# The last gathers ahead of the overflow loop, and a closing norm in two operations a tile

## Chip, cores and metric

One core of a Trainium2 chip runs the program. The metric is the device time of one execution in microseconds (us), as the median of three timed runs. The profile is one more execution, taken with the hardware profiler.

## What is computed

The reference is a network of two blocks over 512 tokens of width 1024, in float32. The first block is attention with a convolution beside it, and then a layer of product-key experts (PEER). The second block has two layers; the second of them ends with a mixture of eight experts (MoE), each token going to two of them, a weighted residual and a layer norm. Only that end is touched here:

```python
def _layernorm(x, g, b):
    xf = x.astype(jnp.float32)
    mu = jnp.mean(xf, axis=-1, keepdims=True)
    var = jnp.mean(jnp.square(xf - mu), axis=-1, keepdims=True)
    return ((xf - mu) * lax.rsqrt(var + LN_EPS) * g.astype(jnp.float32)
            + b.astype(jnp.float32)).astype(x.dtype)

ff = _moe_swiglu(u, w_router, w_gate, w_up, w_down)
x = _layernorm(DEEPNORM_ALPHA * x + (1.0 + g2) * ff, ln2_g[layer], ln2_b[layer])
```

## The kernel before

TensorE (PE) does the matmuls, in three passes of split float32 operands; ScalarE (ACT) and VectorE (DVE) make the splits of the streamed weights (L126, L128); SyncE (SP) issues most transfers; GpSimd (POOL) issues indirect transfers and some small work. The order on PE is the program's own. For the other engines a list scheduler puts the instructions in order when the program is built, and each engine then runs its list in that order.

In `moe` (it ends at L1735) the tokens are written to a buffer in DRAM in rows sorted by expert. A loop over the eight experts (L1700 on) calls `more_rows` or `few_rows`; each result leaves by `store_rows` (L1801: DVE scales it into the tile `yrow`; L1802: POOL stores it to `ybuf`). There are two buffers `ybuf`, one for each half of 512 columns.

The function `gather(h)` (from L1684) brings half h back to token order: for each of the four tiles of 128 tokens two indirect transfers on POOL's queue (L1691, one for each of the token's two experts) into the tile `y`, and two adds on DVE into the residual tile `xt` (L1694, 128x512, one scalar and two tensors). `gather(0)` is called while the last expert's second half is still being multiplied. `gather(1)` needs the store of that second half.

Between the two stands `dense_experts` (L1931, L1932): a loop for tokens that find no room in an expert's rows. Its trip count is read at run time: every engine loads it from the tile `route` (TENSOR_LOAD, L1931) and branches over the loop's body if it is 0, as it is in the runs here. Behind the body stands a block in which each engine waits for the semaphores of all others and of all transfers, before it goes on. The scheduler moves nothing across this loop.

Behind it come `gather(1)`, the statistics of each half row (L1721, `bn_stats`, 8 of them), and the closing norm, two tiles at a time: `bn_aggr` (L1727), an inverse root of 11 small DVE operations (`rsqrt`, L248 to L254), the negated product of mean and root (L1730), then for each tile ACT's scale and shift (L1732), DVE's product with the gain (L1733), DVE's sum with the shift (L1734), all 128x1024, and one store of 512 KB (L1735).

Of the kernel before, what the change touches and what calls it, by code (L numbers as in the profile page):

```python
# [17 lines left out]
AF = mybir.ActivationFunctionType  # L18
OP = mybir.AluOpType
AX = mybir.AxisListType  # L20

P = 128
# [3 lines left out]
NT = 4  # L26
# [1089 lines left out]
LN_EPS = 1e-5  # L1116
# [354 lines left out]
def moe(N, x, acc, last, m2):  # L1471
# [4 lines left out]
    nc, I, sb, tc = N.nc, N.I, N.sb, N.tc  # L1476
    V, A, PE, G = nc.vector, nc.scalar, nc.tensor, nc.gpsimd
# [30 lines left out]
    rows = N.slab([P, 4, D], F32, "rows")  # L1508
# [22 lines left out]
    def area(n, dt=F32):  # L1531
        a = w[:, at[0]:at[0] + n]
        at[0] += n
        return a if dt == F32 else a.bitcast(dt)
# [43 lines left out]
    for t in range(NT):  # L1578
        s = slice(t * NE, (t + 1) * NE)
# [74 lines left out]
    for i in range(2):  # L1654
        for t in range(NT):
            s = G.indirect_dma_start(out=xbuf, out_offset=bass.IndirectOffsetOnAxis(ap=put[:, i, t:t + 1], axis=0),
                                     in_=ut[:, t], in_offset=None, bounds_check=NROWS - 1, oob_is_err=False)
# [24 lines left out]
    xr = [xt[:, t] for t in range(NT)]  # L1682
    bn = area(48).rearrange("p (t h s) -> p t h s", t=NT, h=2)

    def gather(h):

        y = N.slab([P, NT, 2, 512], name="y")
        s = slice(h * 512, (h + 1) * 512)
        for t in range(NT):
            for i in range(2):  # L1690
                G.indirect_dma_start(out=y[:, t, i], out_offset=None, in_=ybuf[h],  # L1691
                                     in_offset=bass.IndirectOffsetOnAxis(ap=get[:, i, t:t + 1], axis=0))
            for i in range(2):
                V.scalar_tensor_tensor(xr[t][:, s], y[:, t, i], gw[:, i, t:t + 1], xr[t][:, s], OP.mult, OP.add)  # L1694
# [19 lines left out]
        behind = late  # L1714
    for f in behind:
        f()
    dense_experts(N, ints[0:1, NE:NE + 1], ud, wd, rows, xr)
    gather(1)
    for t in range(NT):
        for h in range(2):  # L1720
            V.bn_stats(bn[:, t, h], xr[t][:, h * 512:(h + 1) * 512])  # L1721


    mv = area(16).rearrange("p (t s) -> p t s", t=NT)
    for t0 in range(0, NT, 2):
        for t in (t0, t0 + 1):
            V.bn_aggr(mv[:, t, 0:2], bn[:, t])  # L1727
        m = mv[:, t0:t0 + 2]
        rs = N.rsqrt(m[:, :, 1], 2, 1.0, LN_EPS)
        V.scalar_tensor_tensor(m[:, :, 2], m[:, :, 0], -1.0, rs, OP.mult, OP.mult)  # L1730
        for t in (t0, t0 + 1):
            A.activation(xr[t], xr[t], AF.Identity, scale=rs[:, t - t0:t - t0 + 1], bias=mv[:, t, 2:3])  # L1732
            V.tensor_mul(xr[t], xr[t], rows[:, 1])  # L1733
            V.tensor_add(xr[t], xr[t], rows[:, 2])  # L1734
            nc.sync.dma_start(I["out"][t * P:(t + 1) * P], xr[t])  # L1735


def rows_now(N, ut, row, iota):
# [183 lines left out]
def dense_experts(N, trips, ud, wd, rows, xr):  # L1922

    nc, tc, I = N.nc, N.tc, N.I
    V, A, PE, G = nc.vector, nc.scalar, nc.tensor, nc.gpsimd
    y = N.slab([P, KT, T], F32, "dy")
    gu, down = (I["moe_" + k].rearrange("e a p n -> (e a) p n") for k in ("gu", "down"))
    H = 256
    uu = N.slab([P, 2, KT, H], F32R, "du")
    hs = [N.slab([P, 2, 8, H], F32R, "dh") for _ in range(3)]  # L1930
    n = nc.values_load(trips, min_val=0, max_val=NE)  # L1931
    with tc.For_i(0, n) as e:  # L1932
        for hf in range(2):
            ts = slice(hf * H, (hf + 1) * H)
            for k in range(0, KT, 2):
                t = N.tmp([P, 2, H], name="du")
                nc.sync.dma_start(t, ud[:, k:k + 2, ts])
                N.cut(uu[:, 0, k:k + 2], uu[:, 1, k:k + 2], t)
            wr = N.tmp([P, 512], name="dw")
            nc.sync.dma_start(wr[:, 0:H], wd[bass.ds(e, 1), ts].to_broadcast([P, H]))  # L1940
            for f in range(NF):
                ps = [N.ps(), N.ps()]
                for q in range(2):
                    wh, wl = N.split(N.raw_at(gu, e * NF + f, q * 1024))
                    for k in range(4):
                        kk = 4 * q + k
                        for i in range(2):
                            s = slice((2 * k + i) * P, (2 * k + i + 1) * P)
                            N.mm3(ps[i][:, 0:H], wh[:, s], wl[:, s], uu[:, 0, kk], uu[:, 1, kk], kk == 0, kk == KT - 1)
                t = N.tmp([P, 512], name="dg")  # L1950
                A.activation(t[:, 0:H], ps[0][:, 0:H], AF.Silu)
                h = hs[f // 8]
                V.tensor_mul(t[:, 0:H], t[:, 0:H], ps[1][:, 0:H])
                N.cut(h[:, 0, f % 8], h[:, 1, f % 8], t[:, 0:H])
            for q in range(4):
                ps = [N.ps(), N.ps()]
                for a in range(3):
                    m = min(8, NF - 8 * a)
                    for b in range(0, m, 4):
                        wh, wl = N.split(N.raw_at(down, e * 12 + q * 3 + a, b * 256, min(4, m - b) * 256))  # L1960
                        for j in range(min(4, m - b)):
                            f = 8 * a + b + j
                            for i in range(2):
                                s = slice((2 * j + i) * P, (2 * j + i + 1) * P)
                                h = hs[f // 8]
                                N.mm3(ps[i][:, 0:H], wh[:, s], wl[:, s], h[:, 0, f % 8], h[:, 1, f % 8], f == 0, f == NF - 1)
                for i in range(2):
                    V.tensor_mul(y[:, 2 * q + i, ts], ps[i][:, 0:H], wr[:, 0:H])
        for t in range(NT):
            for h in range(2):  # L1970
                p, s = N.ps(), slice(h * 512, (h + 1) * 512)
                for k in range(4):
                    PE.transpose(p[:, k * P:(k + 1) * P], y[:, 4 * h + k, t * P:(t + 1) * P], N.ident)
                r = N.tmp([P, 512], name="yrow")
                V.tensor_mul(r, p, rows[:, 0, s])
                V.tensor_add(xr[t][:, s], xr[t][:, s], r)
# [161 lines left out]
def build(tc, nc, I):  # L2138
    with ExitStack() as ctx:
        N = Net(ctx, tc, I)  # L2140
        N.setup()
        with tc.manual_schedule(engines={mybir.EngineType.PE}):
            with tc.tile_pool(name="early", bufs=1) as N.gp:
                N.gv = N.gp
                x, mods, late, last = mixer1(N)
                (m0, gem0), (m1, gem1) = (modulation(N, l) for l in range(2))
                x, last = peer(N, x, mods, last, (late, gem0(0, 16)))
                start = enter(N, x, last, m0)
            late = ExitStack()
            N.gp = N.late = late.enter_context(tc.tile_pool(name="late", bufs=1))  # L2150
            N.nraw = 6
            N.second()
            with tc.tile_pool(name="gemv", bufs=1) as N.gv:
                N.background("gemv", gem0(16, 48), 2)
                acc, last = mixer2(N, 0, x, *start, m0)
                start = next_input(N, x, acc, last, (0, 4, 7), N.v("ln1_g0"), N.v("ln1_b0"), m0[:, 32:40], m0[:, 24:32])
                N.background("gemv", gem1(0, 48), 1)
                x, acc, last = ffn(N, x, *start, m0)
                N.drain("gemv")
            start = next_input(N, x, acc, last, (0, 2, 3), N.v("ln2_g0"), N.v("ln2_b0"), m1[:, 8:16], m1[:, 0:8])  # L2160
            acc, last = mixer2(N, 1, x, *start, m1)
            late.close()
            N.gp = N.mp = ctx.enter_context(tc.tile_pool(name="moe", bufs=1))
            N.nraw = MOE_RAW
            moe(N, x, acc, last, m1)
# [11 lines left out]
```

## Time and profile before

| what | value |
|---|---|
| median of 3 timed runs | 3920.79 us (3920.43 to 3928.07) |
| time of the profiled execution | 3927.0 us |
| its span, first to last instruction | 3925.1 us |
| PE busy | 3646.8 us, 93% |
| DVE busy | 2897.0 us, 74% |
| ACT busy | 1733.0 us, 44% |
| POOL busy | 989.9 us, 25% |

Times in the rows count from the span's start. The last matmul of the program ends about 36 us before the span does, so what the change touches lies in a stretch in which PE is idle. The profiled execution took 1.9 us more than its span, and 6.2 us more than the median of the timed runs.

### The profile page before, as it was taken

The page shows a single profiled execution, that of the slowest core. Times are in us where ns is not written, and L with a number is a line of the kernel's source. Part 1 is how long each engine was busy: PE and PEld are TensorE (multiplying, and loading weights), DVE is VectorE, ACT ScalarE, POOL GpSimd, SP SyncE. Part 2 cuts the span into 40 slices and gives each one's busy share as a digit, 9 for nine tenths or more (in the row PEclk, how much of TensorE's full clock was granted, in tenths as well). Part 3 has the DMA queues.
Part 4 walks back from the last instruction along what each step waited for, and adds up shares of the span by engine and source line. Part 5 has one row for each costly group of instructions (what it writes and reads, how often), then busy time and mean ns, then how long its engine had stood idle before and what let it go on. Part 6 is the DMA issues. An engine that isn't in the chain of part 4 may idle for free.

```text
span 3925.1 us, 61947 instructions
## 1 busy us (share of the span) xinstructions
PE 3646.8 (93%) x23129; PEld 3331.8 (85%) x23129; DVE 2897.0 (74%) x4938; ACT 1733.0 (44%) x2697; POOL 989.9 (25%) x936
## 2 busy tenths in 40 slices
PE   8999899987999778989999899999999999999996
PEld 5877778887999678889898788888889999999996
DVE  6799866999689766767855755554455788888898
ACT  3355543332444222323333223222324678787775
POOL 2212111054032344555523021002103304031211
PEclk9999999998999889999998999999998999999998
DMA  5322253389599988778864625663124799999997
GB/s 217 98 68 97 95 198 111 102 313 340 179 320 334 360 310 297 288 289 295 303 232 147 193 96 168 188 198 102 60 94 184 262 335 331 339 341 339 338 349 256
DMA packets 314758, 898.97 MB, mean 229 GB/s; under 512 B 28179, under 2 KB 114451, under 8 KB 312783
## 3 DMA queue, kind: packets, MB, share of 16 engines
q1 hardware_dynamic: 273583, 747.68, 55.7%
q0 software_dynamic: 40864, 147.25, 9.9%
q8 instruction: 183, 3.00, 0.3%
q14 instruction: 128, 1.05, 0.1%
HBM read 816.35 MB, written 78.46 MB: 228 GB/s over the span
## 4 chain that ended last, share of the span: by engine, by line
PE 39%; DMA 9%; DVE 6%; issue 5%; POOL 3%; ACT 2%; SPq 0%; DVEq 0%; POOLq 0%; ACTq 0%
PE ps L1819 10%; PE ps L154 9%; PE ps L155 9%; PE ps L153 9%; DMA gw<-Wd 3%; DVE wl L128 2%; DMA raw<-in_peer_v_dram 2%; ACT wh L126 1%; DMA rows<-in_peer_urows_dram,own 1%; DMA raw<-in_ada_w_dram 1%; DVE cw L139 1%; POOL gw L1066 1%; DMA rows<-in_peer_vrows_dram,own 1%; POOL mod L312 1%; DVE raw L331 1%
## 5 line engine op out<-in xcount | busy, mean ns | idle before, releaser
L126 ACT ACTIVATE wh<-raw 128x1024 fp32r<-128x1024 f32 (+1 forms) x1014 | 1050.2, 1042 | 1131.1 <-PE ps L154 594.9
L128 DVE TENSOR_TENSOR wl<-raw,wh 128x1024 fp32r<-128x1024 f32 (+1 forms) x1000 | 1221.5, 1235 | 310.9 <-ACT wh L126 295.0
L155 PE MATMUL ps<-h2h,wl 128*128 128x384 f32 (+2 forms) x1176 | 413.6, 352 | 46.1 <-DVE wl L128 46.1
L153 PE MATMUL ps<-h2h,wh 128*128 128x384 f32 (+2 forms) x1176 | 420.8, 358 | 32.1 <-ACT wh L126 27.7
L155 PE MATMUL ps<-cw,wl 128*128 128x384 f32 (+2 forms) x1088 | 376.0, 346 | 47.2 <-DVE wl L128 47.1
L154 PE MATMUL ps<-h2l,wh 128*128 128x384 f32 (+2 forms) x1176 | 410.2, 349 | 2.3 <-DVE h2l L139 2.1
L153 PE MATMUL ps<-cw,wh 128*128 128x384 f32 (+2 forms) x1088 | 372.5, 342 | 15.9 <-ACT wh L126 15.9
L154 PE MATMUL ps<-cw,wh 128*128 128x384 f32 (+2 forms) x1088 | 371.3, 341 | 0.0
L155 PEld LDWEIGHTS ps<-h2h,wl 128*128 128x128 f32 x1176 | 229.0, 195 | 59.9 <-DVE wl L128 55.1
L154 PE MATMUL ps<-ul,wh 128*128 128x512 f32 (+1 forms) x712 | 269.7, 379 | 8.5 <-DVE ul L139 7.8
L926 POOL DMA_INDIRECT rows<-in_peer_urows_dram,own x128 | 183.6, 1435 | 368.9 <-issue 203.4
L153 PE MATMUL ps<-uh,wh 128*128 128x512 f32 (+1 forms) x712 | 272.6, 383 | 3.4 <-ACT uh L138 2.3
L155 PE MATMUL ps<-uh,wl 128*128 128x512 f32 (+1 forms) x712 | 267.3, 375 | 0.0
L155 PEld LDWEIGHTS ps<-cw,wl 128*128 128x128 f32 x1088 | 215.7, 198 | 58.1 <-DVE wl L128 58.0
L153 PEld LDWEIGHTS ps<-h2h,wh 128*128 128x128 f32 x1176 | 229.6, 195 | 40.2 <-ACT wh L126 30.9
L331 DVE SCALAR_TENSOR_TENSOR raw<-raw,over 128x1024 f32<-128x1024 f32 x128 | 158.5, 1245 | 129.5 <-DMA raw<-in_ada_w_dram 105.3
L154 PEld LDWEIGHTS ps<-h2l,wh 128*128 128x128 f32 x1176 | 229.4, 195 | 7.8 <-DVE h2l L139 3.7
L926 POOL DMA_INDIRECT rows<-in_peer_vrows_dram,own x128 | 165.0, 1289 | 277.0 <-PE ps L971 88.1
L153 PEld LDWEIGHTS ps<-cw,wh 128*128 128x128 f32 x1088 | 215.7, 198 | 18.7 <-ACT wh L126 18.7
L950 DVE SCALAR_TENSOR_TENSOR own<-rows,own 128x1024 f32<-128x1024 f32 x127 | 171.0, 1346 | 74.3 <-DMA rows<-in_peer_vrows_dram,own 73.8
L942 DVE SCALAR_TENSOR_TENSOR rows<-rows,own 128x1024 f32<-128x1024 f32 x128 | 175.2, 1378 | 66.7 <-DMA rows<-in_peer_urows_dram,own 53.1
L1819 PE MATMUL ps<-xe,wh 128*128 128x352 f32 (+3 forms) x1408 | 221.9, 309 | 1.5 <-DVE xe L139 1.5
(529 smaller groups left out, 8579.7 us busy)
## 6 DMA issues: line engine op xcount, KB each, us to landing
raw<-in_moe_gu_dram SPq DMA_DIRECT2D x352, 512.0 KB, 5.8
raw<-in_moe_down_dram SPq DMA_DIRECT2D x160, 512.0 KB, 5.6
raw<-in_peer_v_dram SPq DMA_DIRECT2D x136, 512.0 KB, 6.2
raw<-in_peer_u_dram SPq DMA_DIRECT2D x128, 512.0 KB, 6.5
raw<-in_ada_w_dram SPq DMA_DIRECT2D x96, 512.0 KB, 4.4
raw<-in_w_in_dram SPq DMA_DIRECT2D x88, 512.0 KB, 3.9
Gd<-gelu SPq DMA_DIRECT2D x128, 192.0 KB, 5.4
Wd<-wst SPq DMA_DIRECT2D x12, 2048.0 KB, 14.1
```

The source lines that it names most:

```text
L126: self.nc.scalar.activation(h, src, AF.Copy)
L128: self.lows[-1].tensor_sub(l, src, f32(h))
L139: self.nc.vector.tensor_sub(l, src, f32(h))
L153: mm(out, ah, bh, start=start, stop=False)
L154: mm(out, ah, bl, start=False, stop=False)
L155: mm(out, al, bh, start=False, stop=stop)
L312: self.nc.gpsimd.tensor_scalar(t, x[:, k], sc[:, k:k + 1], sh[:, k:k + 1], OP.mult, OP.add)
L331: V.scalar_tensor_tensor(r, r, 1.0, b, OP.mult, OP.mult, accum_out=out[:, f:f + 1])
L926: G.indirect_dma_start(out=g[:, j], out_offset=None, in_=I[table], in_offset=bass.IndirectOffsetOnAxis(ap=oid[:, a:a + 1], axis=0))
L942: V.scalar_tensor_tensor(g[:, j], g[:, j], 1.0, ox, OP.mult, OP.mult, accum_out=oact[:, a:a + 1])
L950: V.scalar_tensor_tensor(oy, g[:, j], oact[:, a:a + 1], oy, OP.mult, OP.add)
L1819: PE.matmul(ps[j % 2][:, 0:n * (2 - i)], w[i][:, j * P:(j + 1) * P], rs[j // 2][i], start=first and i == 0 and j < 2, stop=last and i == p ...
```

## The change

It does three things. `gather(1)` is called ahead of `dense_experts`, no longer behind it. The norm of a tile is now one DVE operation over 1024 columns, (x - mean) * gain (new L1729), and one more operation for each half of 512 columns, x * root + shift: on DVE (new L1736) for the first halves and both halves of the last tile, and on ACT (new L1733, the product) with POOL (new L1734, the sum) for the second halves of the first three tiles. One chain of inverse roots serves all four tiles, where there were two chains of two tiles. Each half is stored by itself, in 8 transfers of 256 KB (new L1737) where there were 4 of 512 KB. All code behind line 1737 has moved down by two lines.

```diff
--- before.py
+++ after.py
@@ -1714,25 +1714,27 @@
         behind = late
     for f in behind:
         f()
+    gather(1)
     dense_experts(N, ints[0:1, NE:NE + 1], ud, wd, rows, xr)
-    gather(1)
     for t in range(NT):
         for h in range(2):
             V.bn_stats(bn[:, t, h], xr[t][:, h * 512:(h + 1) * 512])
 
 
     mv = area(16).rearrange("p (t s) -> p t s", t=NT)
-    for t0 in range(0, NT, 2):
-        for t in (t0, t0 + 1):
-            V.bn_aggr(mv[:, t, 0:2], bn[:, t])
-        m = mv[:, t0:t0 + 2]
-        rs = N.rsqrt(m[:, :, 1], 2, 1.0, LN_EPS)
-        V.scalar_tensor_tensor(m[:, :, 2], m[:, :, 0], -1.0, rs, OP.mult, OP.mult)
-        for t in (t0, t0 + 1):
-            A.activation(xr[t], xr[t], AF.Identity, scale=rs[:, t - t0:t - t0 + 1], bias=mv[:, t, 2:3])
-            V.tensor_mul(xr[t], xr[t], rows[:, 1])
-            V.tensor_add(xr[t], xr[t], rows[:, 2])
-            nc.sync.dma_start(I["out"][t * P:(t + 1) * P], xr[t])
+    for t in range(NT):
+        V.bn_aggr(mv[:, t, 0:2], bn[:, t])
+    rs = N.rsqrt(mv[:, :, 1], NT, 1.0, LN_EPS)
+    for t in range(NT):
+        V.scalar_tensor_tensor(xr[t], xr[t], mv[:, t, 0:1], rows[:, 1], OP.subtract, OP.mult)
+        for h in range(2):
+            s = slice(h * 512, h * 512 + 512)
+            if h and t < NT - 1:
+                A.activation(xr[t][:, s], xr[t][:, s], AF.Copy, scale=rs[:, t:t + 1])
+                G.tensor_add(xr[t][:, s], xr[t][:, s], rows[:, 2, s])
+            else:
+                V.scalar_tensor_tensor(xr[t][:, s], xr[t][:, s], rs[:, t:t + 1], rows[:, 2, s], OP.mult, OP.add)
+            nc.sync.dma_start(I["out"][t * P:(t + 1) * P, s], xr[t][:, s])
 
 
 def rows_now(N, ut, row, iota):
```

The lists of instructions differ at these places. In them `y_37381` is the tile of `gather(0)`, `y_42061` (before) and `y_37606` (change) that of `gather(1)`, and `route` is a tile with the trip count, the statistics and other small values.

DVE at the entry of the loop, before:

```order
L1694 SCALAR_TENSOR_TENSOR xt_24779<-y_37381,route,xt_24779 128x512 x4
L1801 TENSOR_TENSOR yrow_37603<-ps_37398,rows_24123 128x512
L1694 SCALAR_TENSOR_TENSOR xt_24779<-y_37381,route,xt_24779 128x512 x3
L1931 TENSOR_LOAD route
L1932 COMPARE_AND_BRANCH
L1932 UNCONDITIONAL_BRANCH x2
L2173 BRANCH_PREFETCH_HINT
L139 TENSOR_TENSOR du_37607<-du_37637,du_37607 128x512
```

And in the change:

```order
L1694 SCALAR_TENSOR_TENSOR xt_24779<-y_37381,route,xt_24779 128x512 x4
L1803 TENSOR_TENSOR yrow_37603<-ps_37398,rows_24123 128x512
L1694 SCALAR_TENSOR_TENSOR xt_24779<-y_37381,route,xt_24779 128x512 x3
L1694 SCALAR_TENSOR_TENSOR xt_24779<-y_37606,route,xt_24779 128x512 x8
L1933 TENSOR_LOAD route
L1934 COMPARE_AND_BRANCH
L1934 UNCONDITIONAL_BRANCH x2
L2175 BRANCH_PREFETCH_HINT
L139 TENSOR_TENSOR du_37624<-du_37654,du_37624 128x512
```

The eight adds of `gather(1)` have moved ahead of the load of the trip count.

POOL from the first half's store of the last expert to the end of its list, before:

```order
L1802 DMA ybuf_24103<-yrow_37378 128x512
L1691 DMA y_37381<-ybuf_24103,route 128x512 x8
L1802 DMA ybuf_24104<-yrow_37603 128x512
L1931 TENSOR_LOAD route
L1932 COMPARE_AND_BRANCH
L1932 UNCONDITIONAL_BRANCH x2
L2173 BRANCH_PREFETCH_HINT
L1932 REGISTER_ALU
L1932 COMPARE_AND_BRANCH
L1932 UNCONDITIONAL_BRANCH
L1691 DMA y_42061<-ybuf_24104,route 128x512 x8
```

And in the change:

```order
L1804 DMA ybuf_24103<-yrow_37378 128x512
L1691 DMA y_37381<-ybuf_24103,route 128x512 x8
L1804 DMA ybuf_24104<-yrow_37603 128x512
L1691 DMA y_37606<-ybuf_24104,route 128x512 x8
L1933 TENSOR_LOAD route
L1934 COMPARE_AND_BRANCH
L1934 UNCONDITIONAL_BRANCH x2
L2175 BRANCH_PREFETCH_HINT
L1934 REGISTER_ALU
L1934 COMPARE_AND_BRANCH
L1934 UNCONDITIONAL_BRANCH
L1734 TENSOR_TENSOR xt_24779<-xt_24779,rows_24123 128x512 x3
```

The eight gathers have moved ahead of the load of the trip count, directly behind the store that they read, and three sums of the norm stand behind the loop.

DVE from the end of the loop on, before (the first 11 rows):

```order
L1932 UNCONDITIONAL_BRANCH
L1721 BN_STATS route<-xt_24779 128x6 x4
L1694 SCALAR_TENSOR_TENSOR xt_24779<-y_42061,route,xt_24779 128x512 x2
L1721 BN_STATS route<-xt_24779 128x6
L1694 SCALAR_TENSOR_TENSOR xt_24779<-y_42061,route,xt_24779 128x512
L1727 BN_AGGR route<-route 128x2
L1694 SCALAR_TENSOR_TENSOR xt_24779<-y_42061,route,xt_24779 128x512
L1721 BN_STATS route<-xt_24779 128x6
L1694 SCALAR_TENSOR_TENSOR xt_24779<-y_42061,route,xt_24779 128x512
L1727 BN_AGGR route<-route 128x2
L1694 SCALAR_TENSOR_TENSOR xt_24779<-y_42061,route,xt_24779 128x512
```

And in the change:

```order
L1934 UNCONDITIONAL_BRANCH
L1721 BN_STATS route<-xt_24779 128x6 x8
L1726 BN_AGGR route<-route 128x2 x4
L1729 SCALAR_TENSOR_TENSOR xt_24779<-xt_24779,route,rows_24123 128x1024 x3
L248 TENSOR_SCALAR rsqrt_42090<-route 128x4
L1729 SCALAR_TENSOR_TENSOR xt_24779<-xt_24779,route,rows_24123 128x1024
L249 TENSOR_SCALAR rsqrt_42090<-rsqrt_42090 128x4
L252 SCALAR_TENSOR_TENSOR rsqrt_42090<-rsqrt_42090 128x4
L253 TENSOR_TENSOR rsqrt_42090<-rsqrt_42090 128x4
L254 SCALAR_TENSOR_TENSOR rsqrt_42090<-rsqrt_42090 128x4
L252 SCALAR_TENSOR_TENSOR rsqrt_42090<-rsqrt_42090 128x4
```

Before, the eight statistics alternate with the adds of `gather(1)`; in the change all eight stand in one run behind the loop, ahead of the aggregates, the four wide operations and the one chain of roots, which goes on to five operations L1736 of 128x512. On SP the four stores of 512 KB become eight of 256 KB, in the order of tiles and halves. PE's list is the same in both.

## Rows read from the trace of the kernel before
**Rows 1.** Chain of waits, 3892 to 3898: start us, us, what.

```profile
3892.44 0.09 DVE xt L1694
...
3894.06 0.79 issue
3894.85 3.24 DMA y<-ybuf,route
```

**Rows 2.** Timeline of POOL, 3872 to 3905: start us, us, instruction [idle before].

```profile
3872.83 0.56 POOL L1802 DMA_DIRECT2D ybuf<-yrow  x1 [74.33 <-DVE yrow L1801]
...
3890.70 0.58 POOL L1802 DMA_DIRECT2D ybuf<-yrow  x1 [1.41 <-DVE yrow L1801]
3894.85 0.97 POOL L1691 DMA_INDIRECT y<-ybuf,route  x1 [3.57 <-issue]
...
3903.63 1.35 POOL L1691 DMA_INDIRECT y<-ybuf,route  x1 [0.30 <-issue]
```

**Rows 3.** Transfers, the first and second store to ybuf: us to landing last.

```profile
ybuf<-yrow POOLq DMA_DIRECT2D x1, 256.0 KB, 5.2
...
ybuf<-yrow POOLq DMA_DIRECT2D x1, 256.0 KB, 2.3
```

**Rows 4.** Tile y behind the loop: gather to landing.

```profile
DMA to landing us min/median/max: 3.5/3.8/3.9
```

**Rows 5.** Stores of the result: issue ns, first and last start; landing.

```profile
L1735 SPq DMA_DIRECT2D out_dram<-xt x4: 332/337/348, 3915.7 to 3921.3; - x4
...
DMA to landing us min/median/max: 2.6/2.7/2.8
```

**Rows 6.** Line L1932, 3896.70 to 3898.05: count, ns, first and last start.

```profile
L1932 DVEq EVENT_SEMAPHORE  x12: 49/50/50, 3896.7 to 3897.8; - x12
```

**Rows 7.** Line L1932 over the span: same columns.

```profile
L1932 DVEq EVENT_SEMAPHORE  x13: 21/50/50, 3893.8 to 3897.8; - x13
L1932 PEldq COMPARE_BRANCH  x3: 97/197/3512, 3888.4 to 3894.2; - x3
```

**Rows 8.** DMA queues, 3893.9 to 3896.7: packets, MB, share.

```profile
q14 instruction: 1, 0.01, 0.8%
```

**Rows 9.** Timeline of DVE, 3887 to 3912.

```profile
3887.06 2.73 DVE L1694 SCALAR_TENSOR_TENSOR xt<-y,route,xt 128x512 f32<-128x512 f32 x4
...
3898.08 2.47 DVE L1721 BATCH_NORM_STATS2 route<-xt 128x6 f32<-128x512 f32 x4 [4.89 <-DMA y<-ybuf,route]
...
3903.29 0.20 DVE L1727 BATCH_NORM_AGGREGATE route<-route 128x2 f32<-128x12 f32 x1
3903.41 0.75 DVE L1694 SCALAR_TENSOR_TENSOR xt<-y,route,xt 128x512 f32<-128x512 f32 x1
...
3907.64 0.74 DVE L1694 SCALAR_TENSOR_TENSOR xt<-y,route,xt 128x512 f32<-128x512 f32 x1
...
3910.99 0.16 DVE L252 SCALAR_TENSOR_TENSOR rsqrt<-rsqrt 128x2 f32<-128x2 f32 x1
3911.19 0.16 DVE L253 TENSOR_TENSOR rsqrt<-rsqrt 128x2 f32<-128x2 f32 x1
```

**Rows 10.** Line L331, DVE, two tensors of 128x1024: ns min/median/max.

```profile
L331 DVE SCALAR_TENSOR_TENSOR raw<-raw,over x128: 1200/1225/2312, 80.4 to 2629.5; 128x1024 f32<-128x1024 f32 x128
```

**Rows 11.** Groups of ACT by shape, a 128x512 copy: busy us, mean ns.

```profile
L126 ACT ACTIVATE wh<-raw 128x512 fp32r<-128x512 f32 x32 | 20.2, 631 | 5.7 <-PE ps L155 4.7 <-PE ps L1819 0.7
```

**Rows 12.** Timeline of DVE, 337 to 343.

```profile
337.21 3.35 DVE L503 SCALAR_TENSOR_TENSOR cv<-g,vec,cv 128x505 f32<-128x505 f32 x5
340.49 2.36 DVE L632 TENSOR_TENSOR mx<-mx 128x1 f32<-128x1 f32 x1
```

**Rows 13.** Timeline of POOL in that stretch.

```profile
338.85 3.98 POOL L128 TENSOR_TENSOR wl<-raw,wh 128x1024 fp32r<-128x1024 f32 x1 [15.57 <-ACT wh L126]
```

**Rows 14.** Timeline of POOL and DVE, 2310 to 2313.

```profile
2310.20 1.29 POOL L1194 TENSOR_TENSOR xacc<-xacc,x 128x512 f32<-128x512 f32 x1 [3.88 <-DVE x L1190]
...
2310.21 2.36 DVE L128 TENSOR_TENSOR wl<-raw,wh 128x1024 fp32r<-128x1024 f32 x1 [0.16 <-ACT wh L126]
```


## The prediction, made before the change was run

> **What bounds the kernel now.** PE bounds nearly all of the span, and the change doesn't touch it: its list is the same in both. What can move is the stretch behind the last matmul, some 36 us, so I read that stretch alone: first the chain of waits, then the timelines of POOL and DVE, then the rows of the loop's branch. The chain runs through DVE's last add of the first gather at 3892.44, the loop's entry, POOL's first gather at 3894.85 and so to DVE's statistics [rows 1]. From there to the end it is gathers on POOL and small work on DVE, until the last store is issued at 3921.3, lands 2.8 us later and the span ends 1.0 us after that [rows 5]. So every microsecond here counts in full, in whichever direction.
>
> I measure both versions from one point: the start of the last gathered add on DVE (L1694), 3907.64 before [rows 9]. From there to the end before: 3925.1 - 3907.6 = 17.5 us.
>
> **The gathers ahead of the loop.** They read what the second store to ybuf wrote. It is issued at 3890.70 [rows 2] and lands 2.3 us later [rows 3], at 3893.0. Between the loop's last branch and the first gather POOL needs 0.8 us of its own [rows 1]; I take the same behind the landing, so the first gather starts at 3893.8, where it started at 3894.85 [rows 2]. That is 1.0 us won, and no more: the loop's entry stood beside the landing of the store. The eight gathers keep their pace (3894.85 to 3903.63 for seven steps, 1.25 us each) and their landing of 3.5 to 3.9 us [rows 2, 4]. The last gathered add then starts at 3906.6. Queued behind the gathers on POOL is now the load of the trip count; on DVE the load is behind the adds. POOL reaches it about 3 us before DVE, so DVE is the last engine into the loop.
>
> **The entry of the loop.** This is the term that decides. Before, DVE's last add ahead of the loop starts at 3892.44 and its first instruction behind it at 3898.08: 5.64 us [rows 1, 9]. The profile books 4.89 us of it as a wait for the tile y, and I don't believe that label. The first statistics read the halves of the first gather, and in DVE's order they have nothing between them and the branch. The time that the chain gives to the gather, 3.24 us [rows 1], is less than the shortest landing, 3.5 [rows 4]. And DVE's own queue shows where the time went: of its 13 semaphore waits of the loop the first is at 3893.8, and the other twelve are at 3896.7 to 3897.8 [rows 6, 7]. For 2.9 us the queue did nothing at all, right behind its branch over the body. In that gap one packet of instructions was loaded [rows 8], and PE's branch over its body shows 3.51 us in one record [rows 7]. So it is a jump that waits for its instructions, then a list of waits at 0.1 us each. Before, these 5.64 us lay beside POOL's gathers and cost nothing. Now the adds of these gathers stand ahead of the same jump, nothing is left to hide it, and it costs 5.64 in full: the statistics start at 3912.3.
>
> **The norm.** Before, all of it behind the last gathered add lies in the 17.5 us. Now there stand behind the loop, on DVE one after the other:
> - 8 statistics: four took 2.47 [rows 9], 0.6 each, 4.8 us, to 3917.1. Before, four of them filled DVE's wait for the gathers.
> - 4 aggregates: the next instruction came 0.12 behind one [rows 9]: 0.5 us, to 3917.6.
> - 4 operations of 128x1024 with two tensors: no such operation stands here before. Line L331 has this shape at 1.20 to 1.23 us [rows 10]; two of 128x512 at 0.68 [rows 9] give 1.37 as the upper end. I take 1.2, the same shape: 4.8 us, to 3922.4.
> - the roots: 10 steps that wait for each other, 0.2 us each [rows 9], 2.0 us, to 3924.4. The eleventh lies between the wide operations.
> - 5 operations of 128x512 on DVE, 2.73/4 = 0.68 each [rows 9], 3.4 us. Beside them ACT makes each second half in 0.63 us [rows 11] and POOL adds the shift, three times 1.29 us [rows 14].
>
> Are the last two free of each other? The rows say no. POOL's add at 2310.20 took 1.29 us, and DVE's operation that began with it took 2.36 [rows 14], twice the 1.2 us of two tensors of this shape [rows 10]: it stood until POOL was done. The other way round, an add on POOL took 3.98 us while DVE ran five operations without a gap, 0.67 us each, and then DVE's next one, of a single column, took 2.36 [rows 12, 13]. So POOL, which began in the middle of the five, let the rest of them pass and ran behind them. I take that row, because DVE's five operations here are just such a run: POOL's three adds come behind, 3.4 + 3 x 1.29 = 7.3 us, to 3931.7. The bounds: POOL quite beside DVE, 0.63 + 3.9 = 4.5 us, or after each other with gaps, 8 us.
>
> [...]
>
> **The stores.** SP issues in the order of tiles and halves. The last half on POOL (tile 2) stands ahead of both halves of tile 3, so two stores of 0.34 us [rows 5] follow it: the last is issued at 3932.4. It has 256 KB. Such a store took 2.3 us to ybuf [rows 3], one of 512 KB 2.6 to 2.8 [rows 5]; with three close together I take 2.5: landed at 3934.9, and the end 1.0 later, 3935.9.
>
> **The sum**, against the execution's own span: -1.0 (gathers earlier) + 5.6 (entry uncovered) + 4.8 + 0.5 + 4.8 + 2.0 (DVE up to the last five) + 7.3 + 0.7 + 2.5 + 1.0 (to the end) - 17.5 = **+10.7 us**. The profiled execution took 3927.0 us, 1.9 over its span and 6.2 over the median; against the median the forecast is 3920.8 + 10.7 = **3931.5 us**. About 0.2%, 7.8 us, is what a measurement of this kernel can tell from no change, so this is slower, not by much more than can be told.
>
> **Rivals.**
> 1. *DVE's wait at the loop really was for the gather, as the profile labels it.* Then the entry costs DVE what it cost POOL, which gathers again 0.8 us after its last branch: 3892.44 to 3894.06, 1.6 us, where I put 5.6. That is 4.0 less: +6.7, 3927.5, not slower by what can be told. It decides once 2.9 us (10.7 - 7.8) of the entry go, about the size of the silent gap. For it: the label, and that the numbers meet at 3898.09. Against it: [rows 4, 6, 7]. The same side is reached, at +7.8, if the entry stays but the jump's 2.9 us go. [...] Chance 0.13.
> 2. *POOL and DVE don't disturb each other*: 4.5 in place of 7.3 us, 2.8 less, +7.9, 3928.7, right at the limit. For it: no row has exactly this pair of operations. Against it: [rows 12 to 14]. Chance 0.10.
> 3. *The store lands late.* The first store took 5.2 us [rows 3] under weight loads; the gathers now wait for the second directly. At 5.2 they start 2.9 us later: +13.6, 3934.4. Against it: the weights are all loaded by then. Chance 0.10.
> 4. *It is faster*, since eight wide operations became four and five halves. Even with the entry at 1.6 us and POOL free, the sum stays at +3.9: the statistics and the four wide operations, which now stand behind the loop in one run, take more than is saved. Only the scatter of runs, 7.6 us among the three shown, could show it. Chance 0.04.
>
> The forecast keeps 0.63. **Range:** 3926.5 to 3937.0, from just below rival 1 to rival 3 with the upper ends of POOL's adds and the landing. Slower by over 0.2%: 0.72 (the forecast but for its lower edge, rival 3, half of rival 2); within: 0.24; faster: 0.04.
>
> **What the profile will show.** Right: gathers from about 3893.8; 5.6 us from DVE's last gathered add to its first statistics, with no transfer under way; eight statistics in one run; POOL's adds over 1.3 us or DVE's halves stretched. Wrong: statistics within 2 us of the last add, or POOL's three adds done before DVE's five halves.

## The result, and the profile after it

| | before | after |
|---|---|---|
| median of the timed runs | 3922.76 us (3920.09 to 3928.07, 6 runs) | 3942.94 us (3933.48 to 3953.56, 6 runs) |
| time of the profiled execution | 3927.0 us | 3939.68 us |
| its span | 3925.1 us | 3937.9 us |
| from DVE's last gathered add to the end | 17.5 us | 33.3 us |
| POOL busy | 989.9 us | 998.3 us |

The ratio is 1.0051, with a 95% interval of 1.0033 to 1.0069: slower by 20 us (13 to 27). The forecast was 10.7 us slower, 3931.5 us, and its range ended at 3937.0. The direction was right; the size lies outside the range.

The last row of the table is the stretch in which the prediction made its sum. It grew by 15.8 us, where 11.7 were forecast (the 10.7 and the 1.0 that the earlier gathers were to give back). So I go through that stretch.

First the timeline of POOL in the changed kernel: start us, us, instruction [idle before and what ended it]. It answers to [rows 2].

```profile
3886.95 0.58 POOL L1804 DMA_DIRECT2D ybuf<-yrow  x1 [1.63 <-DVE yrow L1803]
3891.40 0.97 POOL L1691 DMA_INDIRECT y<-ybuf,route  x1 [3.86 <-DMA ybuf<-yrow]
...
3900.81 1.13 POOL L1691 DMA_INDIRECT y<-ybuf,route  x1 [0.30 <-issue]
```

The transfer of that store, us to landing last, as in [rows 3]:

```profile
ybuf<-yrow POOLq DMA_DIRECT2D x1, 256.0 KB, 3.7
```

The gathers now wait for the landing itself: issued at 3886.95, landed 3.7 us later, first gather 0.7 us after that. In the kernel before it landed in 2.3 us [rows 3].

Then the timeline of DVE, which answers to [rows 9]:

```profile
3904.58 0.75 DVE L1694 SCALAR_TENSOR_TENSOR xt<-y,route,xt 128x512 f32<-128x512 f32 x1 [0.62 <-DMA y<-ybuf,route]
3911.72 4.85 DVE L1721 BATCH_NORM_STATS2 route<-xt 128x6 f32<-128x512 f32 x8 [6.39 <-issue]
3916.48 0.41 DVE L1726 BATCH_NORM_AGGREGATE route<-route 128x2 f32<-128x12 f32 x4
3916.81 3.63 DVE L1729 SCALAR_TENSOR_TENSOR xt<-xt,route,rows 128x1024 f32<-128x1024 f32 x3
...
3920.42 1.28 DVE L1729 SCALAR_TENSOR_TENSOR xt<-xt,route,rows 128x1024 f32<-128x1024 f32 x1
3921.62 0.17 DVE L249 TENSOR_SCALAR rsqrt<-rsqrt 128x4 int32<-128x4 int32 x1
...
3923.59 6.42 DVE L1736 SCALAR_TENSOR_TENSOR xt<-xt,rsqrt,rows 128x512 f32<-128x512 f32 x5
```

From the last gathered add to the first statistics it takes 7.14 us, with no transfer of data under way (two packets of instructions, 0.02 MB, are all that moves). Behind that everything stands in one run, as the lists said: statistics 4.8 us, aggregates 0.3, wide operations 4.8, roots 2.0, halves 6.4.

The 7.14 us in the chain of waits (start us, us, what):

```profile
3906.01 0.05 DVEq L1934
3906.06 2.81 issue
3908.87 0.05 DVEq L1934
...
3909.84 0.05 DVEq L1934
3909.89 1.53 issue
3911.42 0.05 DVEq L1934
```

There are two silent stretches, not one. The 2.81 us behind the branch are the jump that was forecast. The 1.53 us lie inside the list of twelve waits, which before ran without a break [rows 6].

The halves on DVE and on POOL by line: count, ns min/median/max, first and last start.

```profile
L1736 DVE SCALAR_TENSOR_TENSOR xt<-xt,rsqrt,rows x5: 746/1742/1758, 3923.6 to 3928.3; 128x512 f32<-128x512 f32 x5
```

```profile
L1734 POOL TENSOR_TENSOR xt<-xt,rows x3: 1700/1706/1732, 3924.4 to 3927.8; 128x512 f32<-128x512 f32 x3
```

DVE's 0.75 us stretch to 1.74 and POOL's add to 1.70, one pair about every 1.7 us: the two take turns. Then the stores on SP, which answer to [rows 5]:

```profile
L1737 SPq DMA_DIRECT2D out_dram<-xt x8: 332/338/433, 3924.4 to 3930.4; - x8
...
DMA to landing us min/median/max: 2.1/2.1/2.3
```

The last one was issued at 3930.4 and landed by 3932.7. Yet the span ends at 3937.9. What stands in those 5.2 us is in the rows of the program's end, where each engine's closing DRAIN is; the first fence is the kernel before, the second the changed one.

```profile
L2173 POOLq DRAIN  x3: 40/109/14787, 3897.8 to 3924.9; - x3
L2173 SPq DRAIN  x3: 7/7/13, 3924.2 to 3924.6; - x3
```

```profile
L2175 POOLq EVENT_SEMAPHORE  x4: 17/17/17, 3937.1 to 3937.8; - x4
L2175 POOLq DRAIN  x3: 40/109/11508, 3925.6 to 3937.7; - x3
L2175 SPq DRAIN  x3: 7/7/13, 3932.9 to 3937.3; - x3
L2175 ACTq EVENT_SEMAPHORE  x2: 17/17/17, 3937.3 to 3937.9; - x2
```

SP reaches its first DRAIN at 3932.9, 0.2 us behind the last landing. POOL's long DRAIN starts at 3925.6 and lasts 11.5 us, to 3937.1, which is 7.6 us after POOL's last add ended (3929.5). Only behind it come POOL's last semaphores (from 3937.1) and those of the others (ACT's from 3937.3), and SP, at its DRAIN since 3932.9, goes on at 3937.3 too. In the kernel before, POOL's last instruction was a gather that ended at 3905.0; the DRAIN ended at 3897.8 + 14.8 = 3912.6, again 7.6 us later, and twelve microseconds before SP's. It was hidden there.

### The profile page after: what moved, and what is told of

It is laid out like the page before. It is cut to its first block, busy times and chain, and to the rows that moved or that the text cites. A ratio compares the mean times of both kernels' runs of the same rounds, so it can differ in the third digit from the quotient of the medians.

```text
span 3937.9 us, 61943 instructions
## 1 busy us (share of the span) xinstructions
PE 3641.7 (92%) x23129; PEld 3326.8 (84%) x23129; DVE 2891.2 (73%) x4926; ACT 1734.1 (44%) x2696; POOL 998.3 (25%) x939
## 5 line engine op out<-in xcount | busy, mean ns | idle before, releaser
L331 DVE SCALAR_TENSOR_TENSOR raw<-raw,over 128x1024 f32<-128x1024 f32 x128 | 158.0, 1240 | 122.7 <-DMA raw<-in_ada_w_dram 98.1
```

The lines of the kernel that those rows point to most:

```text
L331: V.scalar_tensor_tensor(r, r, 1.0, b, OP.mult, OP.mult, accum_out=out[:, f:f + 1])
```

## Experiments

The theory after this reading had three parts: the loop's entry is paid in full, POOL's share of the halves costs some 5.5 us (most of it by the DRAIN), and the norm in two operations is neutral. The main rival: POOL's share costs what the rows of DVE and POOL show, 1.4 us at most, and the rest of the loss is the gather's new place. Each kernel was compared with the kernel before on the same chip; "tail" is the distance from DVE's last gathered add to the end of the span, in the profiled execution (before: 17.5 us).

| kernel | gather(1) | POOL's share | tail, us | against before | ratio (95%) | that is, us |
|---|---|---|---|---|---|---|
| the change | ahead | 3 halves | 33.3 | +15.8 | 1.0051 (1.0033 to 1.0069) | +20 (13 to 27) |
| the change again | ahead | 3 halves | 33.1 | +15.6 | 1.0044 (1.0030 to 1.0057) | +17 (12 to 22) |
| e1_no_pool | ahead | none | 27.6 | +10.1 | 1.0023 (1.0013 to 1.0032) | +9 (5 to 13) |
| e2_gather_back | behind | 3 halves | 20.9 | +3.4 | 1.0013 (1.0003 to 1.0023) | +5 (1 to 9) |
| e3_back_no_pool | behind | none | 15.2 | -2.3 | 1.0000 (0.9990 to 1.0010) | 0 (-4 to 4) |
| e4_gather_only | ahead | none, old norm | 29.0 | +11.5 | 1.0033 (1.0020 to 1.0047) | +13 (8 to 18) |
| e5_drain | behind | 1 column, old norm | 22.4 | +4.9 | 1.0010 (1.0001 to 1.0019) | +4 (0 to 7) |
| e6_no_loop | no loop | 3 halves | 20.8 | +3.3 | 1.0002 (0.9993 to 1.0011) | +1 (-3 to 4) |
| e7_pool_first | ahead | 1 half | 30.0 | +12.5 | 1.0027 (1.0015 to 1.0038) | +11 (6 to 15) |

In every row the tail's growth, read from one execution, lies inside the interval of the times. These intervals are 7 to 14 us wide; so the stretch behind the last gathered add is enough to explain every row, and a difference of a few us ahead of it is not excluded.

### POOL's share taken away

```diff
-            if h and t < NT - 1:
-                A.activation(xr[t][:, s], xr[t][:, s], AF.Copy, scale=rs[:, t:t + 1])
-                G.tensor_add(xr[t][:, s], xr[t][:, s], rows[:, 2, s])
-            else:
-                V.scalar_tensor_tensor(xr[t][:, s], xr[t][:, s], rs[:, t:t + 1], rows[:, 2, s], OP.mult, OP.add)
+            V.scalar_tensor_tensor(xr[t][:, s], xr[t][:, s], rs[:, t:t + 1], rows[:, 2, s], OP.mult, OP.add)
```

> The change, but all eight halves of the norm's second step run on DVE; POOL and ACT have no part in the norm. Theory (POOL's end): in the change the span ends 8.4 us after POOL's last add, not after the last store, because POOL's closing drain takes 7.6 us from its last instruction. Without these adds the drain is over long before, and the span ends with the stores: DVE takes 8 x 0.66 = 5.3 us from the first half, the last store is issued at once, lands 2.3 us later, end 1.0 us on. That is 8.7 us from the first half to the end where the change took 14.3: about 5.5 us faster than the change. Rival (POOL's share is worth having, the end is set elsewhere): 1.4 us faster than the change at most, from 6.8 us to 5.3 us up to the last store, and the same long way from the last store to the end (7.4 us).

3932.38 us. DVE alone needs 5.39 us for all eight halves (timeline of DVE), less than the 6.42 us in which it shared them:

```profile
3921.44 5.39 DVE L1732 SCALAR_TENSOR_TENSOR xt<-xt,rsqrt,rows 128x512 f32<-128x512 f32 x8
```

POOL's long DRAIN of this kernel, by line:

```profile
L2171 POOLq DRAIN  x3: 40/103/7593, 3904.2 to 3929.8; - x3
```

It is over at 3904.2 + 7.6 = 3911.8, eighteen microseconds before the end. The tail is 5.7 us shorter than the changed kernel's, as the theory had it (5.5): 1.4 from the first half to the last store's issue (5.4 for 6.83), the rest because the end follows the stores again (SP's first DRAIN at 3929.2, the end 0.9 us later). The rival, 1.4 us at most, is out.

### The gather put back behind the loop

```diff
-    gather(1)
     dense_experts(N, ints[0:1, NE:NE + 1], ud, wd, rows, xr)
+    gather(1)
```

> The change, but the last gathers stand behind the overflow loop again, as before; the norm in two operations with POOL's share stays. Theory (uncovered loop entry): the statistics lie beside the gathers again and DVE's way through the loop's entry is hidden, so that from the last gathered add to POOL's last add it takes about 11 us, and 8.4 us more to the end through POOL's drain: 19 us, where before took 17.5 and the change 33. About 14 us faster than the change, and 2 us slower than before. Rival (the entry costs little, the change lost its time elsewhere): no more than 5 us faster than the change.

3931.05 us, and the tail 12.4 us shorter than the changed kernel's. The expectation was 14 us. From the last gathered add to POOL's last add it took 12.4 us, not 11, and from there to the end 8.5; the rival, no more than 5 us, is out. POOL's adds stayed at 1.71 us and its DRAIN at 7.6 us behind them:

```profile
L1734 POOL TENSOR_TENSOR xt<-xt,rows x3: 1703/1708/1732, 3916.9 to 3920.3; 128x512 f32<-128x512 f32 x3
```

```profile
L2175 POOLq DRAIN  x3: 40/109/11508, 3918.1 to 3930.2; - x3
```

### Both

> Both edits: last gathers behind the loop as before, and all eight halves of the norm's second step on DVE. Theory: from the last gathered add to the last half about 10.2 us, then 3.4 us to the end: 13.6 us where before takes 17.5: 4 us faster than before, and some 19 us faster than the change. Rival (the norm in two operations gains nothing, since the end hangs on the gathers): within 1 us of before.

The edit is that of the two above together. 3925.52 us, no difference from before within 4 us either way. So the two-operation norm with one chain of roots and stores by halves is neutral in the time as far as can be told; its tail is 2.3 us shorter, less than the interval can show. The 4 us that the theory gave it were not found, and the rival (within 1 us) can't be told from a gain of 2. The timeline of DVE shows what the order behind the loop allows, and the changed kernel lost:

```profile
3904.77 1.28 DVE L1729 SCALAR_TENSOR_TENSOR xt<-xt,route,rows 128x1024 f32<-128x1024 f32 x1
3905.97 0.69 DVE L1721 BATCH_NORM_STATS2 route<-xt 128x6 f32<-128x512 f32 x1
3906.57 0.73 DVE L1694 SCALAR_TENSOR_TENSOR xt<-y,route,xt 128x512 f32<-128x512 f32 x1
...
3913.18 1.28 DVE L1729 SCALAR_TENSOR_TENSOR xt<-xt,route,rows 128x1024 f32<-128x1024 f32 x1
...
3916.34 5.39 DVE L1732 SCALAR_TENSOR_TENSOR xt<-xt,rsqrt,rows 128x512 f32<-128x512 f32 x8
```

Statistics and wide operations stand between the gathered adds. With and without POOL's share the tails differ by 20.9 - 15.2 = 5.7 us here, and by 33.3 - 27.6 = 5.7 us with the gather ahead: the two parts of the loss add up and don't touch each other. No version here beats the kernel before by what can be told.

### The gather alone moved

```diff
+    gather(1)
     dense_experts(N, ints[0:1, NE:NE + 1], ud, wd, rows, xr)
-    gather(1)
```

> The kernel before, with one edit: the last gathers in front of the overflow loop. The old norm stays, so POOL does nothing behind the loop. Theory: the entry (5.6 to 7.1 us) and eight statistics (4.8 us) come behind the last gathered add, then aggregates 0.4, roots 2.8, ACT 1.3, DVE 9.2 and 3.8 us to the end: 28 us where before takes 17.5, less the 1 us or so that the gathers may start earlier (or with a late store 1.6 us later): 9 to 12 us slower than before. Rival (the entry is cheap): 4 to 5 us slower than before.

3934.49 us: on the kernel before, the gather's move alone gives +11.5 us in the tail, within what was expected. It is the larger part of the loss, and the rival (4 to 5 us) is out. DVE's last gathered add and the eight statistics behind it:

```profile
3901.88 0.75 DVE L1694 SCALAR_TENSOR_TENSOR xt<-y,route,xt 128x512 f32<-128x512 f32 x1 [0.86 <-DMA y<-ybuf,route]
3909.11 4.84 DVE L1721 BATCH_NORM_STATS2 route<-xt 128x6 f32<-128x512 f32 x8 [6.48 <-issue]
```

### One column on POOL at the very end

The kernel before, with one line behind its last store:

```diff
+    G.tensor_copy(mv[:, 0, 3:4], xr[NT - 1][:, 0:1])
```

> The kernel before with one small GpSimd operation behind its last VectorE operation: POOL copies one column (128x1) of the last output tile into a spare column, and nothing reads it. Theory 1 (the end of the program waits for POOL's closing DRAIN, which in the profiles so far ends 7.6 us after POOL's last instruction): the last VectorE operation of before ended about 4.9 us ahead of the end of the span; the copy ends some 0.3 us after it, the DRAIN 7.6 us after that, the rest of the end 0.8 us: 3.5 to 5.0 us slower than before, and the trace shows POOL's DRAIN ending behind SP's last instruction. Theory 2 (the DRAIN ends with the program whatever POOL did last, and the 4 us behind the changed kernel's stores come from something else): within 0.5 us of before in the profile's distance from the last VectorE operation to the end, same time.

3933.53 us against 3930.0 before on that chip, and the tail grew by 4.9 us. The timeline around POOL's copy:

```profile
3922.84 2.35 DVE L1734 TENSOR_TENSOR xt<-xt,rows 128x1024 f32<-128x1024 f32 x2
3925.26 0.18 POOL L1736 COPY route<-xt 128x1 f32<-128x1 f32 x1 [16.63 <-DVE xt L1734]
```

And the closing DRAINs:

```profile
L2174 POOLq DRAIN  x3: 40/109/7828, 3925.2 to 3933.6; - x3
L2174 SPq DRAIN  x3: 7/7/13, 3928.1 to 3933.3; - x3
```

A copy of 0.18 us, whose result nothing reads, holds the end of the program back: SP is done at 3928.1, POOL's DRAIN ends at 3925.2 + 7.8 = 3933.1, again 7.6 us after POOL's last instruction. The rival, by which the DRAIN is harmless, is out. The whole price comes from an instruction that runs beside nothing on DVE, whose last operation ended at 3925.19.

### The overflow loop left out

```diff
-    dense_experts(N, ints[0:1, NE:NE + 1], ud, wd, rows, xr)
```

> The changed kernel without the overflow loop: it leaves out the loop for rows over an expert's capacity, whose trip count is 0 with this input. POOL's share of the last halves stays. Theory 1 (the jump into the loop, put behind the gathered adds, costs its own 7.1 us and also keeps the bn_stats and the wide operations from starting between the adds): from the last gathered add to the end 20.9 us as where the gather stands behind the loop, against 33.3 in the changed kernel; the time 3930 to 3932 us, 11 to 13 us under the changed kernel. Theory 2 (only the jump itself is lost, the norm's operations stay in a row): 7 us under the changed kernel, 26 us from the last add to the end. Theory 3 (the place of the gather against PE's end costs, not the loop): within 2 us of the changed kernel.

3928.24 us, 16.4 under the changed kernel of the same set, where 11 to 13 were expected; the tail 20.8 us, 12.3 shorter, as theory 1 put it (20.9). The timeline of DVE from the last gathered add on:

```profile
3904.35 0.74 DVE L1694 SCALAR_TENSOR_TENSOR xt<-y,route,xt 128x512 f32<-128x512 f32 x1
3905.01 1.28 DVE L1720 BATCH_NORM_STATS2 route<-xt 128x6 f32<-128x512 f32 x2
3906.21 0.32 DVE L1725 BATCH_NORM_AGGREGATE route<-route 128x2 f32<-128x12 f32 x2
3906.45 1.27 DVE L1728 SCALAR_TENSOR_TENSOR xt<-xt,route,rows 128x1024 f32<-128x1024 f32 x1
...
3907.70 1.28 DVE L1728 SCALAR_TENSOR_TENSOR xt<-xt,route,rows 128x1024 f32<-128x1024 f32 x1
```

So the loop is worth more than its own entry. From the last add to the first statistics it takes 0.7 us here and 6.9 in the changed kernel of the same set, 6.2 us. The other 6.0 us are work that the loop keeps from starting between the adds: two statistics and two wide operations stand behind the last add here, where the changed kernel has eight and four. Theory 2 (26 us) and theory 3 are out.

### POOL on one half alone

```diff
-            if h and t < NT - 1:
+            if h and t < 1:
```

> The changed kernel with POOL (and ACT) on the second half of the first tile alone; the second halves of the other three go to VectorE, so seven halves there and one on POOL. Theory 1 (POOL's closing DRAIN sets the end): POOL's add ends 3.4 us earlier, its DRAIN too, and the end of the program is then set by the stores again: about 3.4 us less from the last gathered add to the end (30 us for 33.3), 3 to 4 us faster than the changed kernel. Theory 2 (the price is that VectorE and POOL disturb each other, and the DRAIN is harmless): VectorE's last operations take some 0.5 us less in all, and the time is 0.5 us less.

3940.91 us, 3.8 under the changed kernel of the same set, and a tail of 30.0 us as expected. But the stores didn't set the end, as theory 1 had it. POOL's add and the DRAINs:

```profile
3924.80 1.73 POOL L1734 TENSOR_TENSOR xt<-xt,rows 128x512 f32<-128x512 f32 x1 [22.54 <-DVE xt L1736]
```

```profile
L2175 POOLq DRAIN  x3: 40/109/9390, 3924.8 to 3934.7; - x3
L2175 SPq DRAIN  x3: 7/7/13, 3932.1 to 3934.4; - x3
```

The DRAIN ended at 3934.2, 7.6 us after the add, and SP was done at 3932.1. Even the first of POOL's three adds is too late by 2 us. That the DRAIN sets the end is borne out; that it would no longer do so here is not. Theory 2 (0.5 us) is out.

### The changed kernel again

> The changed kernel again, unaltered, on the chip of the other runs of this set, so that they can be compared with it. If its first comparison with the kernel before (20 us by medians, 12.8 us by the two profiled executions) was a fair one, the ratio comes out at 1.005 again. By the sum of the rows of its trace (POOL's DRAIN 4.2 us behind the stores, 1.5 us more at the entry of the loop, the rest as forecast) it is some 13 to 16 us, a ratio of 1.0033 to 1.0041.

3944.66 us against 3930.0: 1.0044, with 1.0030 to 1.0057, which holds both the first ratio and all that the rows gave. The tail is 33.1 us, POOL's long DRAIN lasts 11.51 us as in the first profile of this kernel and ends 0.9 us ahead of the end, and the second gap at the loop's entry is there again with 1.30 us:

```profile
3911.86 1.30 issue
```

The first result was a fair one; whether the change costs 16 or 20 us these runs can't tell.

## Why the prediction was wrong in size

**The last step of the sum failed: "landed at 3934.9, and the end 1.0 later".** It took the end to follow the last store's landing, because it did before. Measured: last store landed 3932.7, end 3937.9, 5.2 us where the step had 1.0. POOL's closing DRAIN had taken the stores' place. Runs e5 (the DRAIN alone, +4.9 us), e1 and e7 show it. The change moved POOL's last instruction from 20.1 us ahead of the end to 8.4 us ahead of it, and I priced that instruction and not what POOL does behind it. The row was in the trace of before: a DRAIN of 14.8 us on POOL that ended 7.6 us after its last gather. I hadn't read the program's last line. What POOL does in these 7.6 us no row shows. SP's DRAINs at the same place take 7 to 13 ns each.

**The entry of the loop: place right, 1.5 us too small.** 5.64 were forecast, 7.14 measured. The silent stretch behind the branch was as read, 2.81 us with nothing else under way but one packet of instructions; that the jump waits for its instructions there is the author's reading of these rows, and no run tested it. Rival 1 (the wait was really for the gather, as the profile labels it) is out. The added 1.53 us lie within the list of waits. All five kernels with the gather ahead show such a gap (1.53, 1.30, 1.33, 1.62, 1.58 us), none of the four with the loop ahead of the gather does. Of the DMA queues in the 1.0 us just ahead of the gap, the instruction queue (packets, MB, share of 16 engines):

```profile
q14 instruction: 1, 0.01, 2.8%
```

One packet of instructions is moved just ahead of the gap, and none in it (3909.89 to 3911.42). A second wait for instructions would be a guess: in the kernel before one is moved at the same place too, during the list of waits (3896.72 to 3898.08), and there is no gap:

```profile
q14 instruction: 1, 0.01, 1.4%
```

So the packet doesn't tell the two orders apart. Why the list runs through when the loop stands ahead of the gather, and so the cause of these 1.5 us, stays open.

**The gathers ahead of the loop: right in kind, and it gave nothing.** POOL did start 0.7 us behind the store's landing (0.8 forecast), but the store landed in 3.7 us, not 2.3, and the gathers went at 1.34 us each (3891.40 to 3900.81), not 1.25. That is part of rival 3. It looks like scatter more than a cost of the change: this store landed in 2.8 and 4.6 us with the gather behind the loop (e3, e2) and in 3.7 to 4.2 with it ahead (the change, e1, e4). And the last gathered add started 19.4 us after the last matmul in the profile of before, 21.5 to 24.1 in the nine others, e5 with the order of before among them (22.0). The 1.0 us was to be won against an execution that happened to be early.

**The norm: right.** Statistics 4.8 (4.8 forecast), aggregates 0.3 (0.5), wide operations 4.8 (4.8), roots 2.0 (2.0). That so many of them stand behind the last gathered add cost 6.0 us, by e6; the prediction had them there.

**POOL and DVE: right that they block each other, the order wrong.** I took the row in which POOL, begun in the middle of five operations, let the rest of them pass [rows 12, 13], 7.3 us and two stores behind it, 8.0 to the last issue. Measured: 6.83 us from the first half to the last issue (3923.59 to 3930.42), because the two alternate, about 1.7 us a pair. POOL's three adds were done (3929.5) before DVE's five halves (3930.0), which the prediction had named as a sign of being wrong. Rival 2 is out. POOL's share was worse than none even so: 6.42 us for five and three, 5.39 us for eight on DVE alone.

The sum with what was measured: 7.14 + 4.76 + 0.33 + 4.81 + 1.97 + 6.83 + 2.3 + 5.2 = 33.3 us, against 17.5. The terms that differ from the forecast are +4.2 (the end), +1.5 (the entry), -1.2 (the halves) and -0.4 (landing and aggregates): 4.1 of the 11.4 us between the forecast (3931.5) and the median (3942.9). Another 1.0 is the gain that the gathers didn't give, and 2.0 is the median of before, 3922.8 over six runs where the forecast stood on 3920.8. That makes 3938.6, outside the range already; the last 4.3 us lie within the interval and stay unexplained. The two profiled spans differ by 12.8 us, less than the tails, because PE's last matmul came at 3883.0 in this execution and at 3888.2 in that of before, and the last gathered add 2.1 us later behind it. That matmul came at 3879.4 to 3889.5 in the ten executions profiled, with the same list on PE, and most of the spread is there at the middle of the list (2262.3 to 2271.1). That spread was not traced further.

## What to carry to other kernels

Before an engine gets work near the end of a program, read the closing rows of that engine, not only of the one that stores last: in all ten profiles here the end came 0.8 to 0.9 us behind the later of two, POOL's long DRAIN and SP's first one, and POOL's ended 7.6 to 7.7 us after its last instruction, be it a gather (before), an add (the change, e2, e7) or a copy (e5), or 7.6 us after its own start where POOL was idle by then (e1, e4). The entry into the loop, which is never run here, left no mark in the tail with POOL's gathers beside it (20.9 us in e2, 20.8 without the loop in e6) and took 6.2 us with nothing beside it. It is also a wall for the order of work: what it keeps apart cost as much here (6.0 us). A distance that was free in one execution (a landing of 2.3 us) is one draw; a gain of that size needs more than one.

## What was not expected of the hardware

- GpSimd's closing DRAIN ends 7.6 to 7.7 us after its last instruction in the five kernels whose rows above show both: after a gather (before), an add of 128x512 (the change, e2, e7) and a copy of one column (e5) alike. In the two without any work of POOL behind the loop and with the gather ahead of it (e1, e4) it lasted 7.59 us from its own start.
- Two engines on one row of halves were slower than one: 6.42 us for five on DVE and three on POOL, 5.39 us for eight on DVE.
- A second silent gap of 1.3 to 1.6 us in a list of semaphore waits behind a jump, in five of five kernels with one order of the code and in none of four with the other.
